# First layer's experts: TensorE's products in one fixed order, the context products in two blocks, and half of each down matrix split into high and low parts

## The chip, the cores and the metric

The program runs on one core of a Trainium2 chip. Its five engines run side by side and wait for each other on semaphores: TensorE (PE, with its weight loads as PEld), VectorE (DVE), ScalarE (ACT), GpSimd (POOL) and SyncE (SP), which here only issues transfers. The metric is the device time of one execution in microseconds (us), the median over the runs shown; less is better.

## What is computed

The reference is a two-layer network over 1024 latent tokens and 256 context tokens of width 1024. Each layer has token mixers and then an expert layer, in which each of 16 experts picks its own tokens (128 latent ones, and 32 context ones in the first layer only) and adds its result to them:

```python
aff = softmax(h @ w_router)
vals, idx = lax.top_k(aff.transpose(0, 2, 1), cap)
xg = h[idx]
hid = silu(xg @ w_gate) * (xg @ w_up)
out = (hid @ w_down) * vals
...
zeros.at[idx].add(out)
```

An expert's three matrices are 1024x512 (gate, up) and 512x1024 (down), in float32. The first layer does this for the latent and for the context tokens; the second layer needs the latent tokens alone.

## The kernel before, in words

Each expert matrix comes as two transfers of 1 MB into a ring of nine `est` tiles (`expert_w`), issued by SP in order; a transfer waits until the tile nine places earlier is free. The products of the latent tokens with gate and up are made from split operands: `split` casts a tile on ACT to a high part `ewh` (float32r) and forms the remainder `ewl` on DVE, in three buffers each; `expert_x` transposes the gathered tokens `xg` on PE (`xt`), scales them on DVE (`xm`), shifts them on POOL, and splits them into `xh` (ACT) and `xo` (DVE). `expert_up` then makes, for each half of a matrix, the twelve products `pg` of xh with ewh, xo with ewh and xh with ewl. The down products `pd` are made in float32 without a split. The 32 context tokens are multiplied in float32 with the `est` tiles themselves, in 32-column strips of the array (`pgc`, `pdc`); their four partial sums are copied to `sc` and added by products with a selection matrix (`hcp`), and the result is transposed (`hct`). `slots` finds the indices of a later expert with small products (`slp`), and POOL gathers by them (`xg`, `xgc`) and scatters the results with an addition (`x<-yo`, `c<-yc`).

The PSUM banks are dealt out by hand (`BANKS`): gate and up sums in banks 0 and 1, the two halves of the down result in 2 and 3, the transposes `xt` and `hidp` in bank 4 alone, the context sums in 5 and 6, `slp` and `xtc` in bank 7.

The order on each engine is set by a scheduler from the order in which the program is written, from the dependencies, and from its own estimate of the times: on PE it puts products of several experts between each other. `issue_after` ties an instruction behind another on its engine. After the last expert the second layer's first modulation vectors are computed (`adaln`, products `aps`), and then the second layer's `norm1` loads the rows of `c` and `x`, squares them on ACT (`sq`), and forms `h`.

Of the kernel before, what the change touches and what calls it, by code (L numbers as in the profile page):

```python
# [19 lines left out]
P = 128  # L20
# [22 lines left out]
class Kern:  # L43
# [1177 lines left out]
    def expert_x(self, l, r, ep, eng=None):  # L1221
# [6 lines left out]
        for k in range(0, KD, 4):  # L1228
            ps = self.bank("xt" if need else "xt2", [P, 4, P], F32, "xt")
            for j in range(4):  # L1230
                nc.tensor.transpose(ps[:, j], xg[:, (k + j) * P:(k + j + 1) * P], self.idf)  # L1231
# [6 lines left out]
        if need:  # L1238
# [4 lines left out]
            for c in range(2):  # L1243
                nc.tensor.transpose(ps[:, c], xgc[:, c * P:(c + 1) * P], self.idf)
# [5 lines left out]

    def expert_up(self, l, r, ep, first=False):
# [4 lines left out]
        pc, sc = None, []  # L1256

        def ctx_mm(gu, hf, st):

            nonlocal pc  # L1260
            if hf == 0:
                pc = self.bank("upc", [P, 512], F32, "pgc")
            for k in range(4):
                kk = 4 * hf + k
                nc.tensor.matmul(pc[32 * k:32 * k + 32], r["xc"][:, kk % 2, 32 * (kk // 2):32 * (kk // 2) + 32],  # L1265
                                 st[:, 512 * k:512 * k + 512], start=hf == 0, stop=hf == 1, tile_position=(0, 32 * k),
                                 skip_group_check=True)
            if hf == 1:
                t = ep.tile([P, 512], F32, name=f"sc{gu}", bufs=1)
                nc.scalar.copy(t, pc)  # L1270
                sc.append(t)
        late = []
        for gu in range(2):
            n = 0
            for hf in range(2):
                st = r[("gate", "up")[gu]][hf]
                wh, wl = r["pre"].pop(0) if r.get("pre") else self.split(self.ws, st, [P, 2048], "ew", 3)
# [5 lines left out]
                if need:  # L1283
                    late.append((gu, hf, st))
                    if len(late) > 1 * first:
                        ctx_mm(*late.pop(0))
        for x in late:
            ctx_mm(*x)
        return acc, sc

    def expert_hid(self, l, r, up, ep):
        nc = self.nc
        need = l < DEPTH - 1
        (pg, pu), sc = up
        hid = ep.tile([P, 512], F32, name="hid", bufs=1 + need)
        nc.scalar.activation(hid, pg, AF.Silu)
        nc.vector.tensor_tensor(hid, hid, pu, ALU.mult)
        ps = self.bank("xt" if need else "downc", [P, 4, P], F32, "hidp")
        for j in range(4):
            nc.tensor.transpose(ps[:, j], hid[:, j * P:(j + 1) * P], self.idf)  # L1300
        hT = ep.tile([P, 4, P], F32, name="hidT", bufs=2)
        nc.scalar.copy(hT, ps)  # L1302
        if need:

            ps = self.bank("downc", [P, 256], F32, "hcp")
# [5 lines left out]
            hc, uc = [ep.tile([64, 256], F32, name=n, bufs=1) for n in ("hidc", "upc")]  # L1311
            nc.scalar.activation(hc, ps[:64], AF.Silu)
            nc.vector.tensor_copy(uc, ps[64:])
            nc.vector.tensor_tensor(hc, hc, uc, ALU.mult)
            ps = self.bank("downc", [P, 2, 64], F32, "hct")
            for c in range(2):
                nc.tensor.transpose(ps[:, c], hc[:, P * c:P * c + P], self.idf[:64, :64])
            hcT = ep.tile([P, 2, 2, 32], F32, name="hcT", bufs=2)
            nc.vector.tensor_copy(hcT.rearrange("p h c s -> p c h s"), ps.rearrange("p c (h s) -> p c h s", h=2))
        return hT, (hcT if need else None)  # L1320

    def expert_down(self, l, r, hid, ep, g5, g5c, xl, xc):
# [6 lines left out]
        for hf in range(2):  # L1329
            st = r["down"][hf]  # L1330

            for k in range(2):
                for nn in range(2):
                    c = 1024 * k + 512 * nn
                    self.downed = nc.tensor.matmul(po[nn], hT[:, 2 * hf + k], st[:, c:c + 512],  # L1335
                                                   start=hf == 0 and k == 0, stop=hf == 1 and k == 1)
            for k in range(2):
                if need:
                    for nn in range(2):
                        o = 64 * k + 32 * nn  # L1340
                        nc.tensor.matmul(pd[o:o + 32], hcT[:, hf, k], st[:, 1024 * k + 512 * nn:1024 * k + 512 * nn + 512],
                                         start=hf == 0, stop=hf == 1, tile_position=(0, o), skip_group_check=True)
# [12 lines left out]
    def experts(self, l, xl, xc):  # L1355

        nc = self.nc
        with self.pool(f"ex{l}") as ep, self.pool(f"ws{l}") as self.ws, self.pool(f"ew3_{l}") as ew3:
# [12 lines left out]
            self.nw = 0  # L1371

# [18 lines left out]
            start(2, rs[0]["xd"])  # L1391
            for e in range(NE):
# [146 lines left out]
```

## Time and profile before

| what | value |
|---|---|
| median of 3 runs | 2729.64 us (2728.22 to 2730.44) |
| the profiled execution | 2732.13 us, span 2730.4 us, so 1.7 us lie around the span |
| PE busy | 2504.4 us (92% of the span) |
| DVE busy | 1884.3 us (69%) |
| ACT busy | 1131.4 us (41%) |
| first layer's experts on PE | first gate product at 1005.67 us, last down product from 1440.27 us on |

The shares are means over stages with different limits; the first layer's experts are about a sixth of the span. A timeline row gives the start, the time from the first start to the last end of a merged group, and in brackets how long the engine had been idle and what ended it. The ends of matmuls are modelled, so for PE the distance between the starts of two neighbouring rows says what a group took.

### The profile page before, as it was taken

How to read it: one execution, taken by the hardware profiler on the slowest of the kernel's cores; microseconds unless marked ns; L12 is line 12 of the kernel's file. 1: busy time of each engine (PE TensorE's matmuls, PEld its weight loads, DVE VectorE, ACT ScalarE, POOL GpSimd, SP SyncE). 2: the span in 40 equal slices, each digit the busy share in tenths (PEclk: the TensorE clock that was granted, in tenths of full speed). 3: DMA queues.
4: the chain of work that ended last, by engine and by line, in shares of the span. 5: the costliest groups of instructions: out<-in, count | busy, mean ns of one | idle time of the engine just before them, and what ended most of it. 6: DMA issues, size and time to landing. Idle time of an engine off the chain costs nothing.

```text
span 2730.4 us, 55190 instructions
## 1 busy us (share of the span) xinstructions
PE 2504.4 (92%) x21959; PEld 1906.9 (70%) x21959; DVE 1884.3 (69%) x4046; ACT 1131.4 (41%) x1878; POOL 669.3 (25%) x621
## 2 busy tenths in 40 slices
PE   7999999998999979999996999999958899589997
PEld 4998887894677855555554988778844677367664
DVE  4258887857666586777754368787858874787874
ACT  4224433324554534444434334333314554345452
POOL 1000000035444633333311000000045532222241
PEclk9999999998999979999998999999979999789999
DMA  7332324247354948888887332423176355889994
GB/s 281 102 108 71 114 68 123 66 138 243 113 160 135 349 151 278 281 280 279 283 280 212 94 105 74 124 84 89 49 200 225 94 163 183 300 281 370 377 376 127
DMA packets 347936, 507.12 MB, mean 186 GB/s; under 512 B 53380, under 2 KB 203072, under 8 KB 346592
## 3 DMA queue, kind: packets, MB, share of 16 engines
q1 hardware_dynamic: 336416, 465.85, 50.4%
q0 software_dynamic: 11264, 37.75, 5.9%
q8 instruction: 173, 2.83, 0.4%
q14 instruction: 83, 0.68, 0.1%
HBM read 410.10 MB, written 94.90 MB: 185 GB/s over the span
## 4 chain that ended last, share of the span: by engine, by line
PE 67%; DVE 18%; DMA 5%; issue 4%; ACT 3%; POOL 2%; SPq 1%; POOLq 0%; DVEq 0%; ACTq 0%
PE pg L1280 13%; PE pj L277 12%; PE pd L1335 8%; PE pj L288 8%; PE po L828 6%; PE nao L786 3%; PE pgc L1265 2%; PE npt L762 2%; PE sA L733 1%; DVE Kt L375 1%; PE aps L157 1%; DVE Kt L376 1%; DVE Qt L378 1%; PE hl L365 1%; PE xt L1231 1%
## 5 line engine op out<-in xcount | busy, mean ns | idle before, releaser
L1182 DVE TENSOR_TENSOR ewl<-est,ewh 128x2048 fp32r<-128x2048 f32 x126 | 298.1, 2371 | 109.7 <-ACT ewh L1178 108.6
L1178 ACT CAST ewh<-est 128x2048 fp32r<-128x2048 f32 x128 | 243.4, 1905 | 170.9 <-PE pg L1280 130.5
L277 PE MATMUL pj<-hl,whi 128*128 128x320 f32 (+2 forms) x912 | 310.2, 340 | 0.0
L277 PE MATMUL pj<-hh,whi 128*128 128x320 f32 (+2 forms) x912 | 309.9, 340 | 0.0
L277 PE MATMUL pj<-hh,wlo 128*128 128x320 f32 (+2 forms) x912 | 308.7, 339 | 0.0
L288 PE MATMUL pj<-whi,hh 128*128 128x256 f32 x960 | 277.8, 290 | 4.5 <-ACT nev L566 4.1
L288 PE MATMUL pj<-whi,hl 128*128 128x256 f32 x960 | 276.8, 291 | 0.8 <-DVE hl L239 0.8
L288 PE MATMUL pj<-wlo,hh 128*128 128x256 f32 x960 | 275.5, 288 | 0.0
L1335 PE MATMUL pd<-est,hidT 128*128 128x512 f32 x512 | 232.2, 596 | 2.1 <-ACT hidT L1302 2.1
L288 PEld LDWEIGHTS pj<-whi,hh 128*128 128x128 f32 x960 | 186.0, 194 | 8.8 <-ACT nev L566 5.2
L288 PEld LDWEIGHTS pj<-wlo,hh 128*128 128x128 f32 x960 | 185.9, 194 | 2.2 <-issue 1.3
L288 PEld LDWEIGHTS pj<-whi,hl 128*128 128x128 f32 x960 | 184.6, 194 | 3.5 <-issue 1.3
L277 PEld LDWEIGHTS pj<-hh,whi 128*128 128x128 f32 x912 | 172.2, 189 | 13.7 <-issue 0.9
L277 PEld LDWEIGHTS pj<-hl,whi 128*128 128x128 f32 x912 | 172.2, 189 | 13.5 <-issue 1.9
L277 PEld LDWEIGHTS pj<-hh,wlo 128*128 128x128 f32 x912 | 172.1, 189 | 13.0 <-issue 1.1
L1335 PEld LDWEIGHTS pd<-est,hidT 128*128 128x128 f32 x512 | 95.2, 189 | 110.7 <-issue 103.3
L265 DVE TENSOR_TENSOR wlo<-wst,whi 128x1024 fp32r<-128x1024 f32 (+1 forms) x72 | 75.2, 1058 | 131.7 <-ACT whi L264 130.6
L1280 PE MATMUL pg<-ewh,xh 128*128 128x512 f32 x512 | 156.8, 424 | 3.1 <-ACT xh L1235 3.0
L752 POOL TENSOR_SCALAR S<-S,sm 128x768 f32<-128x768 f32 (+2 forms) x108 | 108.6, 1007 | 188.3 <-DVE sm L751 166.8
L1280 PE MATMUL pg<-ewl,xh 128*128 128x512 f32 x512 | 147.7, 404 | 0.0
L1280 PE MATMUL pg<-ewh,xo 128*128 128x512 f32 x512 | 142.3, 398 | 2.1 <-DVE xo L1236 2.1
L750 ACT ACTIVATE S<-S,mn 128x768 f32<-128x768 f32 (+2 forms) x108 | 98.6, 913 | 85.2 <-DVE mn L745 79.6
(369 smaller groups left out, 5560.9 us busy)
## 6 DMA issues: line engine op xcount, KB each, us to landing
est<-in_w_exp_gate_dram SPq DMA_DIRECT2D x64, 1024.0 KB
est<-in_w_exp_up_dram SPq DMA_DIRECT2D x64, 1024.0 KB
est<-in_w_exp_down_dram SPq DMA_DIRECT2D x64, 1024.0 KB
wm<-in_w_mod_dram SPq DMA_DIRECT2D x80, 512.0 KB
wst<-in_w_in_dram SPq DMA_DIRECT2D x88, 256.0 KB
pna<-nev SPq DMA_DIRECT2D x180, 64.0 KB
wos<-in_w_out_dram SPq DMA_DIRECT2D x42, 256.0 KB
mst<-mix SPq DMA_DIRECT2D x32, 320.0 KB
```

Source lines behind the costliest of these rows:

```text
L265: nc.vector.tensor_tensor(b, c, a, ALU.subtract)
L277: nc.tensor.matmul(ps[:, :cn], sel(a(k)), b[:, k, c0:c0 + cn], start=n == 0, stop=n == 3 * KD - 1)
L288: nc.tensor.matmul(ps[:, :2 * P], b[:, k, t * P:(t + 1) * P], a(k).rearrange("p a n -> p (a n)"), start=n == 0, stop=n == 3 * KD - 1)
L750: nc.scalar.activation(S[:, :w], S[:, :w], AF.Exp, scale=-1.0, bias=mn[:, 1:2], accum_out=sm[:, 0:1])
L752: nc.gpsimd.tensor_scalar(S[:, :w], S[:, :w], sm[:, 1:2], 1.0, ALU.mult, ALU.mult)
L762: nc.tensor.transpose(pt[:kn, i], S[:, c:c + kn], self.idf)
L786: nc.tensor.matmul(po[64 * X:64 * X + 64, gi], V[:kn, tt, 64 * X:64 * X + 64], PT[X][:kn, i], start=i == 0, stop=i == len(ch) - 1, tile_po ...
L828: nc.tensor.matmul(ps, a, b, start=n == 0, stop=n == len(ops) - 1)
L1178: nc.scalar.copy(hi, src)
L1182: nc.vector.tensor_tensor(lo[:, :m], src[:, :m], hi[:, :m], ALU.subtract)
L1280: nc.tensor.matmul(acc[gu], a[:, 4 * hf + k], b[:, 512 * k:512 * k + 512], start=n == 0, stop=n == 3 * KD - 1)
L1335: self.downed = nc.tensor.matmul(po[nn], hT[:, 2 * hf + k], st[:, c:c + 512], start=hf == 0 and k == 0, stop=hf == 1 and k == 1)
```

## The change

It has four parts, all in the expert layer, and they act in the first layer only (`need` is true there). First, a context manager `then` ties each product and transpose to the one traced before it, so that PE takes them in the order in which they are written. Second, the order written is a new one: within an expert gate, the context's gate and up products together, up; then the context's sums; then the context's down products, the transposes of the expert after next, the latent down products, and the transposes of the hidden values. For the first expert the context's block follows up. Third, the second of the two down tiles is split as gate and up are, and its four float32 products become twelve float32r products, with the hidden values split too (`hTh`, `hTl`). Fourth, banks change: the context's up sums go to bank 6, `hcp` and `hct` to bank 5, and the context's hidden tile is transposed in full width.

```diff
+    @contextmanager
+    def then(self, on=True):
...
+        def after(f):
+            def g(*a, **k):
+                with tc.issue_after(self.pel.ins) if self.pel is not None else nullcontext():
+                    self.pel = f(*a, **k)
+                return self.pel
+            return g
+        nc.tensor.matmul, nc.tensor.transpose = after(mm), after(tr)
...
+        with self.then(need):
+            prods(0)
+            if need and not first:
+                ctx_mm(0)
+                ctx_mm(1)
+            prods(1)
+            if need and first:
+                ctx_mm(0)
+                ctx_mm(1)
...
+            hh, hl = [ep.tile([P, 2, P], F32R, name=n, bufs=2) for n in ("hTh", "hTl")]
+            nc.scalar.copy(hh, hT[:, 2:])
+            nc.vector.tensor_tensor(hl, hT[:, 2:], hh, ALU.subtract)
...
         if need:
+            hTh, hTl = self.hTs
+            wh, wl = self.split(self.ws, r["down"][1], [P, 2048], "ew", 3)
             pd = self.bank("downc", [P, 512], F32, "pdc")
...
+            if mid:
+                mid()
...
+                        if need and hf == 1:
+                            for i, (a, b) in enumerate(((hTh, wh), (hTl, wh), (hTh, wl))):
+                                self.downed = nc.tensor.matmul(po[nn], a[:, k], b[:, c:c + 512], start=False,
+                                                               stop=k == 1 and i == 2)
+                            continue
...
+            hid = self.expert_hid(l, rs[0], up, ep)
+            if need:
+                pc = self.expert_ctx(up[1])
+                hidc = self.expert_ctx_hid(pc, ep)
             for e in range(NE):
                 if e + 3 <= NE:
                     start(e + 3, rs[e + 1]["xd"])
-                hid = self.expert_hid(l, rs[e], up, ep)
-                if e + 2 < NE:
+                if not need and e + 2 < NE:
                     self.expert_x(l, rs[e + 2], self.xp)
                 if e + 1 < NE:
                     up = self.expert_up(l, rs[e + 1], ep)
-                self.expert_down(l, rs[e], hid, ep, g5, g5c, xl, xc)
+                    if need:
+                        pc = self.expert_ctx(up[1])
+                more = lambda: self.expert_x(l, rs[e + 2], self.xp) if e + 2 < NE else None
+                self.expert_down(l, rs[e], (hid, hidc if need else None), ep, g5, g5c, xl, xc, more)
+                if e + 1 < NE:
+                    hid = self.expert_hid(l, rs[e + 1], up, ep)
+                    if need:
+                        hidc = self.expert_ctx_hid(pc, ep)
```

In the order of the changed program every product within `then` bears the line of the wrapper, L1265. The first place is PE around the transposes `xt` of the expert after next, in the middle of the first layer. Before:

```order
L1341 MATMUL pdc<-est,hcT 32x512 x8
L1148 LDWEIGHTS O
L1148 MATMUL slp<-pay,O 128x5
L1148 LDWEIGHTS O
L1148 MATMUL slp<-pay,O 128x5
L1231 MATMUL xt<-idf,xg 128x128 x4
L1280 MATMUL pg<-ewh,xh 128x512
L1280 MATMUL pg<-ewh,xo 128x512 x4
L1280 MATMUL pg<-ewl,xh 128x512 x4
```

And now:

```order
L1265 MATMUL hcp<-sc_13109,sel 32x256 x2
L1265 MATMUL hcp<-sc_13120,sel 32x256 x2
L1265 MATMUL pdc<-est,hcT 32x512 x8
L1265 MATMUL xt<-idf,xg 128x128 x8
L1265 MATMUL xtc<-idf,xgc 128x128 x2
L1265 MATMUL pd<-est,hidT 128x512 x4
L1265 MATMUL pd<-ewh,hTh 128x512
L1265 MATMUL pd<-ewh,hTl 128x512
L1265 MATMUL pd<-ewl,hTh 128x512
```

Before, gate and up products stood between the two groups of four transposes; now the eight follow each other, though both groups use bank 4. The second place is DVE at the same point of an expert. Before (`A` is the scale of the tokens):

```order
L1154 SCALAR_TENSOR_TENSOR ix<-sl,pdiv 128x1
L1156 SCALAR_TENSOR_TENSOR ixd<-sl,pdiv 128x1
L1233 TENSOR_TENSOR xm<-xt,A_12256 128x512
L1351 TENSOR_TENSOR yd<-pdc,yd 64x512
L1352 SCALAR_TENSOR_TENSOR yc<-yd,val,g5c 64x512
```

And now:

```order
L1182 TENSOR_TENSOR ewl<-est,ewh 128x2048
L1349 TENSOR_TENSOR hid<-hid,pg 128x512
L1182 TENSOR_TENSOR ewl<-est,ewh 128x2048
L1333 COPY upc<-hcp 64x256
L1234 TENSOR_TENSOR xm<-xt,A_12256 128x512
L1404 TENSOR_TENSOR yd<-pdc,yd 64x512
L1334 TENSOR_TENSOR hidc<-hidc,upc 64x256
L1405 SCALAR_TENSOR_TENSOR yc<-yd,val,g5c 64x512
```

Two splits (those of the next gate), the product `hid` and a copy now stand directly ahead of the first `xm`. The third place is PE at the first expert, after the small products `slp`. Now:

```order
L1265 MATMUL xtc<-idf,xgc 128x128 x2
L1265 MATMUL xt<-idf,xg 128x128 x8
L1265 MATMUL xtc<-idf,xgc 128x128 x2
L1265 MATMUL pg<-ewh,xh 128x512 x4
L1265 MATMUL pg<-ewh,xo 128x512 x4
```

Before, at this place:

```order
L1280 MATMUL pg<-ewl,xh 128x512 x4
L1231 MATMUL xt<-idf,xg 128x128 x4
L1280 MATMUL pg<-ewh,xh 128x512 x4
L1244 MATMUL xtc<-idf,xgc 128x128 x2
L1280 MATMUL pg<-ewh,xo 128x512 x4
```

The first expert's products `pg` used to start ahead of the second expert's transposes; now they stand behind them.

## Rows read from the trace of the kernel before

**Rows 1.** Windows: stretch, its us, five engines' busy us, PE clock, DMA share, GB/s.

```profile
1000.00:1020.00 20.00, 16.39 (x67) 12.13 (x67) 18.00 (x32) 7.08 (x6) 5.15 (x3) 0.65 0.21 66
1200.00:1250.00 50.00, 50.00 (x265) 27.57 (x263) 36.57 (x48) 22.27 (x23) 18.29 (x12) 1.00 0.83 282
```

**Rows 2.** Chain in order of time: start, us, what; first and last of eleven.

```profile
1100.55 4.29 PE pd L1335 x10
...
1372.87 4.29 PE pd L1335 x10
```

**Rows 3.** Timeline of PE, one expert of the middle.

```profile
1182.09 4.45 PE L1335 MATMUL pd<-est,hidT 128*128 128x512 f32 x10
1186.47 1.92 PE L1265 MATMUL pgc<-est,xct 128*32 128x512 f32 x16
1188.32 2.84 PE L1335 MATMUL pd<-est,hidT 128*128 128x512 f32 x6
...
1198.71 0.64 PE L1231 MATMUL xt<-idf,xg 128*128 128x128 f32 x4
1199.10 0.48 PE L1280 MATMUL pg<-ewh,xh 128*128 128x512 f32 x1
1199.41 1.08 PE L1280 MATMUL pg<-ewh,xo 128*128 128x512 f32 x4
1200.33 1.07 PE L1280 MATMUL pg<-ewl,xh 128*128 128x512 f32 x4
...
1204.93 0.64 PE L1309 MATMUL hcp<-sc,sel 128*32 128x256 f32 x8
```

**Rows 4.** Timelines of ACT, DVE and POOL, the same expert.

```profile
1200.53 1.91 ACT L1178 CAST ewh<-est 128x2048 fp32r<-128x2048 f32 x1 [1.17 <-PE pg L1280]
...
1183.01 0.43 DVE L1313 COPY upc<-hcp 64x256 f32<-64x256 f32 x1
...
1199.38 0.69 DVE L1233 TENSOR_TENSOR xm<-xt,A 128x512 f32<-128x512 f32 x1
...
1202.78 2.29 DVE L1182 TENSOR_TENSOR ewl<-est,ewh 128x2048 fp32r<-128x2048 f32 x1
1204.99 0.69 DVE L1236 TENSOR_TENSOR xo<-xm,xh 128x512 fp32r<-128x512 f32 x1
...
1202.92 3.48 POOL L1170 DMA_INDIRECT c<-yc,ixd  x1 [0.83 <-DVE val L1160]
```

**Rows 5.** Timelines of PE and POOL, first two experts.

```profile
1002.08 1.12 PE L1231 MATMUL xt<-idf,xg 128*128 128x128 f32 x4 [0.78 <-DVE xm L1233]
...
1005.67 3.75 PE L1280 MATMUL pg<-ewh,xh 128*128 128x512 f32 x8
...
1018.67 0.60 PE L1231 MATMUL xt<-idf,xg 128*128 128x128 f32 x4
...
1012.51 1.69 POOL L1165 DMA_INDIRECT xg<-h2l,ix  x1 [0.30 <-DVE xo L1236]
1017.52 2.83 POOL L1165 DMA_INDIRECT xgc<-h2c,ix  x1 [3.33 <-DVE ixd L1156]
```

**Rows 6.** Timelines of PE, POOL, SP and ACT, from the last expert to the second layer.

```profile
1440.27 7.13 PE L1335 MATMUL pd<-est,hidT 128*128 128x512 f32 x16 [0.73 <-ACT hidT L1302]
...
1448.65 4.49 PE L157 MATMUL aps<-est,sT 128*32 128x512 f32 x40
1453.07 0.33 PE L1317 MATMUL hct<-idf,hidc 64*128 64x64 f32 x2
...
1455.89 1.90 PE L1341 MATMUL pdc<-est,hcT 128*32 128x512 f32 x16
...
1461.07 1.43 POOL L1170 DMA_INDIRECT c<-yc,ixd  x1 [10.49 <-DVE yc L1352]
...
1466.43 0.97 SPq L221 DMA_DIRECT2D x<-c  x2
...
1472.35 1.06 ACT L224 ACTIVATE sq<-x 128x1024 f32<-128x1024 f32 x1 [0.24 <-DMA x<-c]
...
1477.42 1.94 ACT L236 ACTIVATE h<-ps,mt,ab 128x256 f32<-128x256 f32 x4
```

More of the change, by code (lines that the diff above doesn't have):

```diff
@@ L1255, in expert_up, with prods @@
         acc = [self.bank("up", [P, 512], F32, "pg") for _ in range(2)]
[L1256 to L1273, printed above, removed]
+        sc = []
+        def prods(gu):
             n = 0
             for hf in range(2):
-                st = r[("gate", "up")[gu]][hf]
-                wh, wl = r["pre"].pop(0) if r.get("pre") else self.split(self.ws, st, [P, 2048], "ew", 3)
+                wh, wl = r["pre"].pop(0) if r.get("pre") else self.split(self.ws, r[("gate", "up")[gu]][hf], [P, 2048],
+                                                                         "ew", 3)
                 for a, b in ((xh, wh), (xo, wh), (xh, wl)):
@@ L1282, in expert_up, with ctx_mm, expert_ctx @@
                         n += 1
[L1283 to L1288, printed above, removed]
+        def ctx_mm(gu):
+            pc = self.bank(("upc", "downc")[gu], [P, 512], F32, "pgc")
+            for hf in range(2):
+                st = r[("gate", "up")[gu]][hf]
+                for k in range(4):
+                    kk = 4 * hf + k
+                    nc.tensor.matmul(pc[32 * k:32 * k + 32], r["xc"][:, kk % 2, 32 * (kk // 2):32 * (kk // 2) + 32],
+                                     st[:, 512 * k:512 * k + 512], start=hf == 0, stop=hf == 1, tile_position=(0, 32 * k),
+                                     skip_group_check=True)
+            t = ep.tile([P, 512], F32, name=f"sc{gu}", bufs=1)
+            nc.scalar.copy(t, pc)
+            sc.append(t)
+        with self.then(need):
+            prods(0)
[6 more added lines that the diff above has]
+                ctx_mm(1)
         return acc, sc
-    def expert_hid(self, l, r, up, ep):
+    def expert_ctx(self, sc):
         nc = self.nc
[L1293 to L1305, printed above, removed]
+        ps = self.bank("upc", [P, 256], F32, "hcp")
+        with self.then():
             for i, t in enumerate(sc):
@@ L1318, in expert_hid, with expert_ctx_hid @@
[L1318 to L1322, printed above, removed]
+        return ps
+    def expert_ctx_hid(self, ps, ep):
+        nc = self.nc
+        hc, uc = ep.tile([P, 256], F32, name="hidc", bufs=1), ep.tile([64, 256], F32, name="upc", bufs=1)
+        nc.scalar.activation(hc, ps, AF.Silu)
+        nc.vector.tensor_copy(uc, ps[64:])
+        nc.vector.tensor_tensor(hc[:64], hc[:64], uc, ALU.mult)
+        pt = self.bank("upc", [P, 2, P], F32, "hct")
+        with self.then():
+            for c in range(2):
+                nc.tensor.transpose(pt[:, c], hc[:, P * c:P * c + P], self.idf)
+        hcT = ep.tile([P, 2, 2, 32], F32, name="hcT", bufs=2)
+        nc.vector.tensor_copy(hcT.rearrange("p h c s -> p c h s"), pt[:, :, :64].rearrange("p c (h s) -> p c h s", h=2))
+        return hcT
@@ L1323, in expert_down @@
+    def expert_down(self, l, r, hid, ep, g5, g5c, xl, xc, mid=None):
         nc = self.nc
@@ new lines, in expert_down @@
+            if mid:
+                mid()
+        po = [self.bank("down", [P, 512], F32, "pd") for _ in range(2)]
+        with self.then(need):
+            for hf in range(2):
+                for k in range(2):
+                    for nn in range(2):
+                        c = 1024 * k + 512 * nn
+                        if need and hf == 1:
[3 more added lines that the diff above has]
+                            continue
+                        self.downed = nc.tensor.matmul(po[nn], hT[:, 2 * hf + k], r["down"][hf][:, c:c + 512],
+                                                       start=hf == 0 and k == 0, stop=hf == 1 and k == 1)
```

62 lines of the change are left out of this document (40 added, 22 removed).

## The prediction

> **What bounds the kernel now.** I read the page first (PE 92% of the span), then windows of 20 and 50 us over the first layer's experts, the chain of waits for the period, and the timelines of one expert and of both ends. In the middle of these experts PE is busy for 50.00 of 50 us at a granted clock of 1.00, while DVE has 36.57, ACT 22.27 and POOL 18.29, and the DMA engines are used to 0.83 at 282 GB/s [rows 1]. So PE sets the pace there, and nothing waits for weights. In the chain the same group `pd` comes at 1100.55 and, ten experts on, at 1372.87 [rows 2]: the period is 272.32 / 10 = 27.23 us. At the start it is otherwise: PE has 16.39 of 20 us and a clock of 0.65 [rows 1]. At the end no expert follows, and the path runs through the last scatters and the loads of the second layer's rows. So three places are to be costed: the start, the period (14 of them matter), and the crossing into layer two.
>
> **The period, PE's own work.** Sixteen `pd` records are the eight down products; ten take from 1182.09 to 1186.47, 0.438 each [rows 3], so 7.01 us in all. After the change eight records stay (3.50) and twelve float32r products come. These cost as `pg` does: four from 1199.41 to 1200.33, 0.23 each [rows 3], together 2.76. That saves 0.75 us. A lone `pg` behind the transposes took 0.31 (1199.10 to 1199.41) against 0.23 [rows 3], so a change of kind costs about 0.08; the fixed order has some four fewer, -0.3, while the small `slp` products, which are not tied, fall into the context block (+0.15 estimated). PE's work per expert is then 27.23 - 0.75 - 0.30 + 0.15 = 26.33 us. Were PE never to wait, 15 experts would gain some 13 us.
>
> **The new wait.** Both transposed halves `xt` use bank 4, and nothing stands between them now: the second four wait until DVE's `xm` has read the first. In the middle it does not occur before, since `pg` lay between. And `xm` will not start at once: DVE's order now has two `ewl`, `hid` and `upc` ahead of it. I count from the end of the xo products of up's first half, which frees the buffer of the next `ewh`:
>
> - ACT's cast starts 0.20 later and takes 1.91 (1200.33 to 1200.53; [rows 3, 4]).
> - `ewl` 2.21: its start to the next one's, 1202.78 to 1204.99 [rows 4]. Back to back, DVE's 2.29 overlaps the next by 0.08.
> - `hid`, of the shape of `xm` (0.69), taken as 0.61; the second `ewl` 2.21; `upc` 0.43 less 0.08; `xm` 0.69 [rows 4].
>
> At the start, where two groups of `xt` did follow each other, the wait is seen: 0.78 us on DVE `xm` [rows 5].
>
> The sum of the list is 2.11 + 2.21 + 0.61 + 2.21 + 0.35 + 0.69 = 8.18 us. In that time PE has four wl products (0.92), up's second half (12 x 0.23 = 2.76), `hcp` 0.64, `pdc` 1.90 and the first `xt` 0.64, each of these three less some 0.05 since their ends are modelled [rows 3, 6]: 6.71 us. PE waits 1.5 us per expert. The lower bound is a DVE that is free: then the wait is about 0.95 (the 0.78 of the start with the transposes' own tail). The upper bound is 2.1, if both `ewl` run without overlap and the cast is late by half a microsecond. I take 1.5, because DVE's order is a fixed queue and each term is a row. The period is 26.33 + 1.5 = 27.85, about **27.9 us** (27.3 to 28.4), +0.65 over 14 experts: about +9 us.
>
> The Trainium skill, "Perfetto Trace Analysis", section "Matmuls", says that independent matmul groups should rotate through different PSUM banks, so that the reading out of one overlaps the next. It speaks against the two halves back to back in one bank, and the 0.78 us of [rows 5] agrees with it. By that rule alone, without DVE's queue, the wait would be the 0.95 of the lower bound.
>
> **What is hidden.** The split of the down tile adds a cast of 1.91 on ACT and an `ewl` of 2.29 on DVE per expert [rows 4]. ACT has 22.27 of 50 busy and DVE 36.57 [rows 1], about 19.9 of 27.23 for DVE; with 2.3 and `hTl` more (a quarter of a tile's width, at most 0.5) it is 22.7 of 27.9. The d1 split can be done while PE is at gate and up, some ten us ahead of its use; if its cover went, PE would wait up to 4.2 us per expert, which no load supports. Five splits go through three buffers instead of four; each buffer comes free at least 9 us before its next products. Weights: 282 GB/s at a share of 0.83 leaves room for 340, and a longer period asks for less. The `est` tile of the split is held until its `pdc` and the split are through, no longer than before.
>
> **The start.** The order now ties the second expert's transposes ahead of the first `pg`. Their rows `xg` are gathered by an instruction on POOL that starts at 1012.51, and they stood ready at 1018.67, where `xt` ran without a wait [rows 5]. POOL's place for that gather doesn't move. `xgc`, which started at 1017.52 after 3.33 us of waiting for its index [rows 5], follows at once now, as the index products no longer stand behind `pg`. So the first half starts near 1018.2, then `xm` 0.69 and the second half 0.60, and `pg` starts near 1020.3 instead of 1005.67 [rows 5]. If the gathers land 1 us sooner or 3 later, so does it. Of the 48 `pg`, the first dozen go at the low level of the clock (0.47 each, 3.75 for eight, against 0.23 [rows 3, 5]; the clock was 0.65 on average in this stretch [rows 1]): 11.0 + 2.9 + 0.4. Two context blocks follow, 1.85 each (1186.47 to 1188.32, [rows 3]), to 1038.3. Then come the copy of the sums, `hcp` 0.64, silu, `upc` 0.43, the product and `hct` 0.33 [rows 3, 4, 6], about 4.1 with waits that aren't covered (2.1 is the bare sum with 0.69 for the copy; 6 if ACT and DVE are at splits). The second expert's gate starts near 1042.4.
>
> **The crossing.** The last down product ends at 1042.4 + 14 x 27.9 - 0.5 (the first period has no earlier down ahead) + 24.8 (the fifteenth has neither `xt` nor `slp`, nor the wait) + 9.7 (the sixteenth: 1.4 wait for `hcT`, 1.85 `pdc`, 6.45 `pd`) = **1467**. Before it was 1440.27 + 7.1 = 1447.4 [rows 6]. So PE is 20 us later there, but most of it comes back. Before, the last `hct` and `pdc` stood behind the 40 `aps` (1448.65, 1453.07, 1455.89), the scatter `c` ran at 1461.07, the load of these rows at 1466.43, `sq` at 1472.35 and `h` at 1477.42, 30 us after the last `pd` [rows 6]. Now `pdc` stands ahead of `pd`, the context rows are scattered during `pd`, and the path is that of `x`: its scatter goes 1.1 after the last `pd`, and as with `c` (1461.07 to 1466.43) its rows can be loaded 5.4 later; from there to `h` it took 10.99 at most (1466.43 to 1477.42), and 0.97 + 5.07 at least [rows 6]. So `h` is 12.5 to 17.5 behind the last `pd`. I take 15.7, as SP's queue has the load of the modulation vectors ahead of `x`'s rows, and those wait for `aps` (4.4 us) and the sums behind it. `h` starts at 1482.7, +5.3; with the weights of the first projection queued behind those loads I take +6.
>
> **The sum.** +6.0 on the profiled execution of 2732.13, i.e. 2738.1. That execution is 2.49 above the median of 2729.64, so on the runs' scale 2735.6: **2736 us**. Counted otherwise: start and crossing give back what they take to about -3, and the period adds 9. The second layer is untouched but for the order of some small products; +-3 us unpriced. 0.2%, 5.5 us, is about what a measurement of this kernel can tell from no change, so the forecast lies just outside of it.
>
> **Rivals.**
> - *The wait is shorter than what is saved (faster).* Place: DVE before `xm`. If `xm` gets ahead of an `ewl`, or the cast starts sooner, 2.2 us leave the chain and only a remnant of 0.45 stays: period 26.8, 14 x 1.1 = 15.4 less than forecast: 2720; without any wait 2714. It decides from a wait of about 0.65 down (2736 - 14 x 0.85 = 2724). For it: PE's own work falls by 0.9 for certain. Against it: DVE's order is fixed, and even a free DVE costs 0.95 by the row.
> - *The wait is at its floor (no change).* 0.95: period 27.3, 2736 - 14 x 0.6 = 2727.6, within 0.2%.
> - *A second wait per expert (slower still).* POOL's scatter `c` stands between the two additions to `xm`. It took 3.48 us beside a split on DVE [rows 4] and 1.43 alone [rows 6]. If it takes the long form here each time, the second half's `xh` and `xo` come 2 us later, where about 1 is to spare: +1.0 per expert, 2750. The Trainium skill, "SBUF — State Buffer", section "Who interferes with whom", says that DVE and GpSimd share a port pair under an exclusive lock, which fits the two durations.
> - *The fixed order does nothing* since the scheduler had it so: excluded by the order, which differs at all three places.
>
> **How the numbers follow.** Forecast 0.55 (2729 to 2743: the wait from 1.1 to 2.0, crossing and start +-3), second wait 0.18, shorter wait 0.17, floor 0.10. The range runs from 2718, which takes in most of the shorter wait, to 2750. Faster by over 0.2% (below 2724) is the shorter wait and a little of the floor: 0.20. Within 0.2% (to 2735): the floor's rest and the lower half of the forecast, 0.33. Slower: the forecast's upper half and the second wait, 0.47.
>
> **What would show it.** The period between equal `pd` groups: 27.9; 26.8 or less means that the wait is gone, 28.9 that there are two. PE idle 1.5 us ahead of the second `xt`, ended by DVE `xm`, with two `ewl` just before. `pg` of the first expert at 1020, the second's gate at 1042. The last `pd` at 1467 and `h` 15 to 16 us later. The prediction is wrong if DVE comes to `xm` early, if the gathers of the start are late, or if d1's split is late, which would show as PE waiting for DVE `ewl` ahead of `pd`.

## The result, and the profile after

The changed kernel takes 2765.8 us in the median of 4 runs (2762.62 to 2766.76), the kernel before 2730.04: a ratio over all runs of 1.0117 (95% interval 1.0103 to 1.0132; the plain quotient of the two medians is 1.0131). It is slower, in the direction of the forecast, but by 36 us in the medians and 32 by the ratio, where 6 were predicted. The profiled execution has a span of 2765.0 us against 2730.4.

The windows of the middle of the first layer's experts, as in [rows 1]: stretch, its us, busy us of PE, PEld, DVE, ACT and POOL, PE clock, DMA share, GB/s.

```profile
1150.00:1200.00 50.00, 46.58 (x248) 27.60 (x248) 41.93 (x54) 23.18 (x23) 18.38 (x12) 0.97 0.79 249
1200.00:1250.00 50.00, 46.39 (x259) 29.44 (x257) 40.38 (x47) 24.73 (x25) 15.82 (x11) 1.00 0.83 281
```

PE no longer is busy throughout, and in one of the two windows its clock is below 1. The chain of waits, which in [rows 2] ran through PE alone, now leaves it once per expert for DVE:

```profile
1181.22 7.72 PE pd L1265 x20
...
1207.03 2.20 DVE ewl L1182
1211.34 6.21 PE pd L1265 x20
...
1235.62 2.20 DVE ewl L1182
...
1413.14 7.83 PE pd L1265 x20
```

From one `ewl` of the chain to the next it is 28.59 us, the period, where 27.23 stood before and 27.85 was forecast. Three of the `pd` groups (the third starts at 1297.15) take 7.7 to 7.8 us instead of 6.2: around each of them a window of 50 us reads a granted clock of 0.97 (of the two levels, 1.2 and 2.4 GHz, the lower for a part of it), where all windows of these experts read 1.00 before.

The timeline of PE, two experts of the middle and one near the end, with ACT and DVE behind it:

```profile
1208.02 0.66 PE L1265 MATMUL xt<-idf,xg 128*128 128x128 f32 x4
1210.47 0.66 PE L1265 MATMUL xt<-idf,xg 128*128 128x128 f32 x4 [1.79 <-DVE xm L1234]
...
1223.96 2.76 PE L1265 MATMUL pgc<-est,xct 128*32 128x512 f32 x18
1226.65 0.20 PE L1148 MATMUL slp<-pay,O 128*128 128x5 bf16 x2
1226.79 1.92 PE L1265 MATMUL pgc<-est,xct 128*32 128x512 f32 x14
1228.63 1.20 PE L1265 MATMUL pg<-ewh,xh 128*128 128x512 f32 x4
...
1427.06 3.64 PE L1265 MATMUL pgc<-est,xct 128*32 128x512 f32 x32
1430.63 1.20 PE L1265 MATMUL pg<-ewh,xh 128*128 128x512 f32 x4
...
1432.57 1.07 PE L1265 MATMUL pg<-ewl,xh 128*128 128x512 f32 x4
...
1438.58 0.66 PE L1265 MATMUL xt<-idf,xg 128*128 128x128 f32 x4
1441.04 0.65 PE L1265 MATMUL xt<-idf,xg 128*128 128x128 f32 x4 [1.81 <-DVE xm L1234]
...
1432.77 1.91 ACT L1178 CAST ewh<-est 128x2048 fp32r<-128x2048 f32 x1 [1.42 <-PE pg L1265]
...
1434.71 2.29 DVE L1182 TENSOR_TENSOR ewl<-est,ewh 128x2048 fp32r<-128x2048 f32 x1 [4.22 <-ACT ewh L1178]
1436.92 0.68 DVE L1349 TENSOR_TENSOR hid<-hid,pg 128x512 f32<-128x512 f32 x1
1437.52 2.28 DVE L1182 TENSOR_TENSOR ewl<-est,ewh 128x2048 fp32r<-128x2048 f32 x1
1439.84 0.43 DVE L1333 COPY upc<-hcp 64x256 f32<-64x256 f32 x1
1440.29 0.69 DVE L1234 TENSOR_TENSOR xm<-xt,A 128x512 f32<-128x512 f32 x1
```

Two things are to be seen. First, the forecast wait: the second `xt` starts 2.45 us behind the first, 1.8 of it idle, and DVE works through `ewl`, `hid`, `ewl` and `upc` without a pause before it comes to `xm`. Second, one that the prediction had priced at 0.15 us: the context block of the middle, with two `slp` in it, lasts from 1223.96 to 1228.63, 4.67 us; the same 32 products without `slp`, near the end, last from 1427.06 to 1430.63, 3.57 us.

Start and crossing, the rows that answer to [rows 5, 6], from the timelines of POOL, PE, SP and ACT:

```profile
1016.02 1.87 POOL L1165 DMA_INDIRECT xg<-h2l,ix  x1 [0.30 <-DVE ix L1154]
...
1021.22 1.12 PE L1265 MATMUL xt<-idf,xg 128*128 128x128 f32 x4 [2.90 <-DMA xg<-h2l,ix]
1024.32 2.06 PE L1265 MATMUL pg<-ewh,xh 128*128 128x512 f32 x4
...
1044.99 2.06 PE L1265 MATMUL pg<-ewh,xh 128*128 128x512 f32 x4
...
1443.39 1.46 POOL L1170 DMA_INDIRECT c<-yc,ixd  x1 [1.22 <-DVE yc L1405]
...
1481.53 7.07 PE L157 MATMUL aps<-est,sT 128*32 128x512 f32 x64
...
1488.66 0.80 SPq L221 DMA_DIRECT2D x<-c  x2
...
1498.50 1.93 ACT L236 ACTIVATE h<-ps,mt,ab 128x256 f32<-128x256 f32 x4
...
1502.45 0.79 PE L288 MATMUL pj<-whi,hh 128*128 128x256 f32 x2 [1.28 <-ACT whi L264]
```

And behind the crossing, in the second layer, which the change doesn't touch: the products `atp` (three groups of modulation vectors, the last in the second layer's attention) and the router's products `lgk` behind that attention, first of before, then of the changed kernel (the last numbers ahead of the shapes are first and last start):

```profile
L171 PE MATMUL atp<-idf,ms x24: 272/273/422, 32.9 to 2109.9; 128*128 128x128 f32 x24
...
L942 PE MATMUL lgk<-hT,wm x128: 272/273/297, 2314.5 to 2352.2; 128*32 128x128 f32 x128
```

```profile
L171 PE MATMUL atp<-idf,ms x24: 272/273/328, 34.7 to 2138.2; 128*128 128x128 f32 x24
...
L942 PE MATMUL lgk<-hT,wm x128: 272/273/297, 2349.6 to 2387.2; 128*32 128x128 f32 x128
```

At the second layer's first projection `pj` the changed kernel is 23.5 us behind (1502.45 against 1478.99 before), at the last `atp` 28.3, and at `lgk` 35.1. So a third of the loss arises in code that both kernels share. (The last `atp` stands 33 products further ahead of `lgk` in the changed kernel's order, so the part up to it and the part behind it are best taken together: `pj` to `lgk` takes 11.6 us more than before.)

### The profile page after: what moved, and what is told of

It is laid out like the page before. It is cut to its first block, busy times and chain, and to the rows that moved or that the text cites. A ratio compares the mean times of both kernels' runs of the same rounds, so it can differ in the third digit from the quotient of the medians.

```text
span 2765.0 us, 55363 instructions
## 1 busy us (share of the span) xinstructions
PE 2506.5 (91%) x22023; PEld 1937.4 (70%) x22023; DVE 1934.0 (70%) x4078; ACT 1171.2 (42%) x1910; POOL 669.1 (24%) x621
## 4 chain that ended last, share of the span: by engine, by line
PE 64%; DVE 18%; DMA 7%; ACT 4%; issue 3%; POOL 2%; SPq 2%; POOLq 0%; ACTq 0%; DVEq 0%
PE pj L277 12%; PE pj L288 7%; PE pg L1288 6%; PE po L828 6%; PE pg L1265 5%; PE pd L1265 4%; PE pd L1394 4%; PE nao L786 3%; PE pgc L1265 2%; DVE ewl L1182 2%; PE npt L762 2%; PE aps L157 2%; DMA wm<-in_w_mod_dram 2%; PE sA L733 1%; ACT ewh L1178 1%
## 5 line engine op out<-in xcount | busy, mean ns | idle before, releaser
L1182 DVE TENSOR_TENSOR ewl<-est,ewh 128x2048 fp32r<-128x2048 f32 x142 | 330.8, 2334 | 126.5 <-ACT ewh L1178 124.9
L1178 ACT CAST ewh<-est 128x2048 fp32r<-128x2048 f32 x144 | 274.2, 1908 | 166.6 <-PE pg L1288 81.8
L1235 POOL TENSOR_TENSOR xm<-xm,mt 128x512 f32<-128x512 f32 x60 | 80.8, 1356 | 208.8 <-DVE xm L1234 194.9
L157 PE MATMUL aps<-wm,sT 128*32 128x512 f32 x320 | 85.0, 672 | 41.3 <-DMA wm<-in_w_mod_dram 41.3
L786 PE MATMUL nao<-PT,nav 128*64 128x128 f32 (+1 forms) x1296 | 114.9, 286 | 5.8 <-ACT PT L765 5.3
L354 ACT COPY kz<-Kt 64x320 f32<-64x320 f32 x120 | 55.0, 467 | 150.4 <-DVE Kt L375 131.0
L1394 PE MATMUL pd<-est,hidT 128*128 128x512 f32 x256 | 115.1, 592 | 0.7 <-ACT hidT L1355 0.7
```

The lines of the kernel that those rows point to most:

```text
L157: nc.tensor.matmul(ps[32 * j:32 * j + 32], self.sT[:, k, :], w[j], start=k == 0, stop=k == KD - 1, tile_position=(0, 32 * j))
L786: nc.tensor.matmul(po[64 * X:64 * X + 64, gi], V[:kn, tt, 64 * X:64 * X + 64], PT[X][:kn, i], start=i == 0, stop=i == len(ch) - 1, tile_po ...
L1178: nc.scalar.copy(hi, src)
L1182: nc.vector.tensor_tensor(lo[:, :m], src[:, :m], hi[:, :m], ALU.subtract)
L1394: self.downed = nc.tensor.matmul(po[nn], hT[:, 2 * hf + k], r["down"][hf][:, c:c + 512], start=hf == 0 and k == 0, stop=hf == 1 and k == 1)
```

## The experiments

Each ratio is to the kernel before in runs of the same chip, whose median was 2727.7 to 2733.78 us on the four chips; a difference between two other kernels is across chips unless the text says otherwise. Kernels whose name begins with "halves" differ from the changed kernel, the rest as said. The period is taken from `hidp` to `hidp` over ten experts.

**The halves of xt kept apart.** The second four transposes go behind the four float32 `pd` products.

```diff
-            if mid:
-                mid()
+            if mid:
+                mid((0,))
...
             for hf in range(2):
+                if need and hf == 1:
+                    mid((4,))
```

> The changed kernel with the second group of four xt transposes moved behind the four float32 pd products, so that PE has other work while xm reads the first group out of bank 4; nothing else differs. Theory 1 (the wait for xm is what lengthens the period, 1.81 us idle per expert in the changed kernel, and the drops of the clock inside the experts follow from PE's idling): no idle time ahead of the second xt, period 28.59 down to about 26.7, no 3.4 us drop of the clock between the second expert and the last, time 2765.8 - 14 x 1.9 - 3 x 1.5 = about 2735. Rival (the fixed order only moves the wait: the next thing PE needs, hTl, the split of the down tile or ewl of the next gate, is late by as much): period stays above 28, time above 2757.

Measured: 2714.24 us, a ratio of 0.9949 (0.9932 to 0.9965) to before: faster than both kernels. PE's timeline:

```profile
1117.92 0.60 PE L1266 MATMUL hidp<-idf,hid 128*128 128x128 f32 x4
...
1212.60 0.66 PE L1266 MATMUL xt<-idf,xg 128*128 128x128 f32 x4
...
1213.31 3.60 PE L1266 MATMUL pd<-est,hidT 128*128 128x512 f32 x8
1216.75 0.60 PE L1266 MATMUL xt<-idf,xg 128*128 128x128 f32 x4
...
1226.37 3.64 PE L1266 MATMUL pgc<-est,xct 128*32 128x512 f32 x32
1229.94 1.21 PE L1266 MATMUL pg<-ewh,xh 128*128 128x512 f32 x4
...
1373.09 0.60 PE L1266 MATMUL hidp<-idf,hid 128*128 128x128 f32 x4
```

No wait is left, and the period is (1373.09 - 1117.92) / 10 = 25.52. The rival falls: nothing else is late. But it gains 51.6 us on the changed kernel (49 when each is held against before on its own chip) where theory 1 expected 30, since the period fell by 3.07 and not by 1.9. The wait is 2.1 of it (counted from start to start, the two `xt` groups cost 2.95 us per expert before this edit and 0.85 after). The other 1.0 is the context block: the scheduler, which places the free `slp`, now puts them elsewhere, and the block takes 3.57 us. The drops of the clock are gone with the wait. What two different banks for the two halves would bring was not tried.

**No split.** All down products in float32 again, order and banks as changed.

```diff
-            wh, wl = self.split(self.ws, r["down"][1], [P, 2048], "ew", 3)
...
-                        if need and hf == 1:
-                            for i, (a, b) in enumerate(((hTh, wh), (hTl, wh), (hTh, wl))):
...
-            hh, hl = [ep.tile([P, 2, P], F32R, name=n, bufs=2) for n in ("hTh", "hTl")]
...
```

> The changed kernel with all down products in float32 again (no split of the second down tile, no hTh and hTl); order and banks as changed. Theory 1 (the split saves PE 0.8 us per expert but its fifth place in the ring of three ew buffers makes the casts of the next gate wait for up's last products, so that two ewl stand ahead of xm): pd 7.0 instead of 6.2, but the casts go early and the wait for xm falls from 1.8 to about 0.9; period about 28.3 to 28.5, time 2758 to 2765. Rival (the split is a plain gain of PE and the wait comes from the order alone): the wait stays at 1.8, period 29.4, time about 2777.

Measured: 2774.72 us, 1.0169 (1.0141 to 1.0196). The rival holds:

```profile
1214.18 0.86 PE L1265 MATMUL xt<-idf,xg 128*128 128x128 f32 x4 [1.80 <-DVE xm L1234]
```

The wait is as long as with the split, and the period is 29.2 us, or 30.9 where the clock drops, which it does in five periods. A cast goes as soon as the xo products three splits earlier have freed its buffer, with four splits per expert as with five, so two `ewl` fall ahead of `xm` in either case. The wait does not come from the split.

**Free start.** The second expert's transposes are written behind the first expert's products.

```diff
-            self.expert_x(l, rs[1], self.xp)
...
             with self.tc.issue_after(slotted.ins), self.tc.issue_after(self.listed.ins):
                 up = self.expert_up(l, rs[0], ep, True)
+            if need:
+                self.expert_x(l, rs[1], self.xp)
```

> The changed kernel with the second expert's transposes written behind the first expert's products instead of ahead of them; the rest differs in nothing. Theory 1 (the start costs because the first pg stand behind transposes that wait for their gathers): the first pg starts some 13 to 15 us earlier than in the changed kernel, the second expert's gate 8 to 12 us earlier, time about 2754 to 2758. Rival (the start is bound by the gathers and by the second expert's own transposes, so that the second gate starts when it did): time within 4 us of 2765.8.

Measured: 2762.32 us, 1.0127 (1.011 to 1.0144), 3.5 us below the changed kernel across chips; against before, each on its own chip, the two are about equally slow.

```profile
1010.94 2.04 PE L1265 MATMUL pg<-ewh,xh 128*128 128x512 f32 x4
...
1036.66 2.06 PE L1265 MATMUL pg<-ewh,xh 128*128 128x512 f32 x4
```

The first `pg` starts 13.4 us earlier than in the changed kernel, the second expert's gate 8.3, but this execution was 7.0 us ahead already at the router's first `ctp` (981.3 against 988.3), in code that has the same order in both. Of the start itself 1.3 us remain. The rival holds: the transposes, the sums and `hct` that now stand between the two experts take what the early start gives.

**The split alone**, in the kernel before.

```diff
+            wh, wl = self.split(self.ws, r["down"][1], [P, 2048], "ew", 3)
...
+                    if need and hf == 1:
+                        for i, (a, b) in enumerate(((hTh, wh), (hTl, wh), (hTh, wl))):
```

> The kernel before with the split of the second down tile alone (twelve float32r products in place of four float32 ones, hidden values split too); the scheduler orders everything, no banks change. Theory 1 (PE is the bound and the split takes 0.75 us of its work per expert, its cast and its ewl hidden): period 27.23 to 26.5, time 2730 - 11 = about 2719. Rival (five splits in a ring of three buffers make ACT and DVE late, or the scheduler's order gets worse, and PE waits as it does in the changed kernel): period 27.2 or more, time 2730 or more.

Measured: 2740.6 us, 1.0042 (1.0025 to 1.0059): slower. The windows of this kernel over 300 us of the experts:

```profile
1100.00:1400.00 300.00, 300.00 (x1629) 166.31 (x1628) 237.45 (x300) 152.44 (x154) 99.29 (x64) 1.00 0.83 277
```

PE is busy for 300 of 300 us at a clock of 1, and yet the period of these ten experts is (1388.92 - 1109.51) / 10 = 27.94 against 27.23. The down products `pd` fall from 7.08 to 6.51 us per expert, but the scheduler breaks the other products up: `pgc` comes in 4.5 groups per expert and costs 4.53 us (3 groups and 3.85 before), `pg` comes in 7.3 groups in place of 5 and costs 12.11 in place of 11.77, `pdc` costs 2.17 in place of 1.86. Neither theory had this: PE doesn't wait, it works worse. The order isn't the same in all experts: from the first `hidp` to the last, 15 periods, this kernel takes 414.4 us and before 412.8, so the split's saving is used up and little more. Of the 9.6 us by which the profiled execution is longer, 2.3 are there ahead of the experts and 7.2 lie in the second layer (below).

**A small part of the change that should cost nothing**: the full-width `hct` alone (with the silu ahead of it over 128 rows), in the kernel before.

```diff
-            ps = self.bank("downc", [P, 2, 64], F32, "hct")
+            ps = self.bank("downc", [P, 2, P], F32, "hct")
...
-                nc.tensor.transpose(ps[:, c], hc[:, P * c:P * c + P], self.idf[:64, :64])
+                nc.tensor.transpose(ps[:, c], hc[:, P * c:P * c + P], self.idf)
```

> The kernel before with one small part of the change alone: the context's hidden tile is transposed in full width (hct 128x128 in place of 64x64). In the first layer this is some 0.1 us per expert of PE's work or nothing, but the scheduler's order of the second layer's attention preparation becomes the one of the changed kernel (on SP two loads of qk ahead of four wm in place of qk, wm, qk, three wm). Theory 1 (the changed kernel's second layer, about 10 us longer than before, is longer because of that order): this kernel is 6 to 10 us slower than before, all of it behind the point where the second layer prepares the second pair of heads. Rival (the second layer's 10 us come from the first layer's late end, from another phase of clock drops, or are chance): within 3 us of before.

Measured: 2741.0 us, 1.0036 (1.0022 to 1.005): slower by some 10 us. The windows from the second layer's first `pj` to its first `lgk`, of before, of this kernel and of the changed one, in the columns of [rows 1]:

```profile
1478.99:2314.54 835.55, 766.64 (x8375) 636.23 (x8375) 592.35 (x1392) 336.60 (x664) 163.54 (x165) 0.97 0.41 125
```

```profile
1479.01:2324.36 845.35, 773.03 (x8376) 641.03 (x8376) 590.21 (x1392) 336.72 (x664) 161.18 (x165) 0.97 0.41 124
```

```profile
1502.45:2349.60 847.15, 776.43 (x8369) 643.20 (x8369) 588.70 (x1385) 336.79 (x662) 162.40 (x165) 0.96 0.41 124
```

Its first layer is as short as before's (`h` at 1477.41 against 1477.42). From `pj` to `lgk` it takes 9.8 us more than before, and the order on the engines there, the attention's above all, is nearly the changed kernel's. Theory 1 holds, and for the change as a whole it means that most of the second layer's loss has nothing to do with how long the experts take. The windows also show how this order lengthens the stretch: PE is busy 6.4 us longer for the same products, and 9.8 us in the changed kernel. In the trace's records of the granted clock the lower level holds for 43 us of this stretch before, 55 here and 64 in the changed kernel; half of the added time, 6 and 10 us, is an estimate of what that costs at most. So most of the loss is the granted clock, and the rest is PE idling. The changed kernel's order gives no fixed loss, though: by their profiled executions, halves apart and free start, with the same order, are 9.1 and 5.1 us longer than before from `pj` to `lgk`.

**The slot products kept out of the context block**, in the changed kernel.

```diff
-                if e + 3 <= NE:
-                    start(e + 3, rs[e + 1]["xd"])
...
                     up = self.expert_up(l, rs[e + 1], ep)
+                    if need and e + 3 <= NE:
+                        self.tie = self.ctxl
+                        start(e + 3, rs[e + 1]["xd"])
+                        self.tie = None
```

with each `slp` behind `self.tie`, the last product of the context block.

> The changed kernel with the slot products slp of the expert three ahead kept behind the context block (they go behind up and between the two xt groups); nothing else is moved by hand. Theory 1 (two slp products in the middle of the strip products pgc break the groups of four that run side by side, 4.54 us per block in place of 3.57): pgc falls to 3.6 us, the period by about 1 us, time about 2752. Rival (the longer block is a wait for banks or data that only happens to stand beside the slp): pgc stays at 4.5, time within 4 us of 2765.8.

Measured: 2740.43 us, 1.0041 (1.0026 to 1.0055).

```profile
1212.15 3.64 PE L1266 MATMUL pgc<-est,xct 128*32 128x512 f32 x32
1215.72 1.20 PE L1266 MATMUL pg<-ewh,xh 128*128 128x512 f32 x4
...
1224.36 0.20 PE L1149 MATMUL slp<-pay,O 128*128 128x5 bf16 x2
1226.27 0.66 PE L1266 MATMUL xt<-idf,xg 128*128 128x128 f32 x4 [1.72 <-DVE xm L1235]
```

The block takes 3.57 us again with the wait still there, as theory 1 had it. The period is (1369.52 - 1096.81) / 10 = 27.27, 1.3 below 28.59: 1.0 is the block, and the rest small pieces: two `slp` now run inside the wait, the other eight no longer stand within a run of `pg`, and the wait is 0.1 shorter. The gain is 25 us across chips and not 14. The profiled executions differ by 28.3: 3.3 are there ahead of the experts, 20.4 arise from there to the second layer's first projection (14 x 1.3 = 18, and no drop of the clock is left in the middle), and 4.6 behind it, where the order is another one.

**xm ahead of the splits on DVE**, in the changed kernel: the next gate's two `ewl` are tied behind the first `xm`.

```diff
+            with self.tc.issue_after(self.low.ins) if self.low is not None else nullcontext():
+                nc.vector.tensor_tensor(lo[:, :m], src[:, :m], hi[:, :m], ALU.subtract)
...
+                self.low = self.xm0 if need and not first and gu == 0 else None
```

> The changed kernel with the next gate's two ewl tied behind the first xm on DVE; transposes stay back to back in bank 4. Theory 1 (the wait is DVE's queue, 8.5 us of ewl, hid, ewl and upc from the end of up's first xo products, and the bank alone costs only about 0.95): the second xt waits 0.8 to 1.0 us in place of 1.81, period about 27.6 to 27.8, time 2750 to 2754. Rival (bank 4 itself or the late upc sets it): the wait stays above 1.5 us, time within 5 us of 2765.8, or slower as the next gate's ewl is late.

Measured: 2792.23 us, 1.0226 (1.0211 to 1.0241).

```profile
1214.47 0.65 PE L1268 MATMUL xt<-idf,xg 128*128 128x128 f32 x4 [0.79 <-DVE xm L1235]
...
1228.02 2.05 PE L1268 MATMUL pg<-ewh,xo 128*128 128x512 f32 x4 [2.16 <-DVE xo L1240]
```

The wait ahead of the second `xt` falls to 0.79, the floor of the start's row in [rows 5]. So the other microsecond was DVE's queue. But the two `ewl` now stand ahead of the second `xm`, `xo` is late, and PE waits 2.16 us at the next gate, behind which `pg` runs at half clock (four in 1.84 us in place of 0.91). The period is (1405.68 - 1098.60) / 10 = 30.71. The time contradicts the expectation, the place of the wait confirms it. The context block of this kernel has `slp` in it too, eight of them, but behind 24 strip products:

```profile
1231.63 2.78 PE L1268 MATMUL pgc<-est,xct 128*32 128x512 f32 x24
1234.35 0.36 PE L1148 MATMUL slp<-pay,O 128*128 128x5 bf16 x8
1234.63 1.07 PE L1268 MATMUL pgc<-est,xct 128*32 128x512 f32 x8
```

Here the 32 strip products take 3.72 us (2.72 and 1.00 from start to start), not 4.54. So a product over the full array in the block is not by itself what costs; in the changed kernel the two `slp` come behind 18 strip products, the last two of which run singly.

**Halves apart, and no split.** Both edits above.

> The changed kernel with the xt halves apart (as in halves_apart) and all down products in float32. Theory 1 (with PE never waiting the split is worth its PE time, 7.0 - 6.2 = 0.8 us per expert): period 25.5 + 0.8 = 26.3, time 2714 + 13 = about 2727, if the second layer keeps its length. Rival (the split's cast and ewl cost elsewhere as much as PE saves): period 25.5 to 25.8, time 2714 to 2718.

Measured: 2727.46 us, 0.9987 (0.9978 to 0.9996). The period is (1382.91 - 1120.99) / 10 = 26.19, 0.67 above that with the split; theory 1 holds. This kernel makes the same products as the one before but for the wider `hct`, and PE waits in neither; the order, with the banks that go with it, takes the period from 27.23 to 26.19. By kind of product, per expert, `pg` falls from 11.77 to 11.39 us, `pgc` from 3.85 to 3.57, `pd` from 7.08 to 6.87, `hct` from 0.27 to 0.14 (the width), `hcp` from 0.57 to 0.46.

**Halves apart, with the narrow hct of before**, for another order of the second layer.

```diff
-        pt = self.bank("upc", [P, 2, P], F32, "hct")
+        pt = self.bank("upc", [P, 2, 64], F32, "hct")
...
-                nc.tensor.transpose(pt[:, c], hc[:, P * c:P * c + P], self.idf)
+                nc.tensor.transpose(pt[:, c], hc[:, P * c:P * c + P], self.idf[:64, :64])
```

> halves_apart with the context's hidden tile transposed in 64 columns again, as in the kernel before. In the first layer nothing but some 0.1 us per expert can change; the scheduler's order of the second layer becomes a third one, unlike that of before and of the changed kernel. Theory 1 (the order of the second layer is worth some 8 us by itself, whatever the experts do): experts as in halves_apart, period 25.5, and a second layer that differs from that of halves_apart by several us in either direction; time between 2704 (as short as before's) and 2720. Rival (that stretch is long whenever the first layer ends at another time): the same 8 us as in halves_apart, 2714 within 2 us.

Measured: 2726.66 us beside 2733.78 for before on this chip, 0.9971 (0.9961 to 0.9981), so 0.2% less gain than with the full width. The period is 25.74, 0.22 more (in full width, `hct` and the `hidp` ahead of it cost 0.2 less), and the second layer is 3 us longer still in the one execution profiled. Theory 1 holds in that the order alone changes that stretch; that it would get as short as before's it did not.

## Why the prediction was wrong

The span grew by 34.6 us, where 6.0 were forecast. By places: 3.6 are there already at the router's first `ctp`, 19.9 arise from there to the second layer's first projection, and 11.1 behind it. Against the forecast, the period is 14 x 0.74 = 10.4 too long, the drops of the clock add 5, the crossing 3 and the second layer 11.1; the start, with the first and last experts, gives back some 4.

**Ahead of the experts, 3.6 us, forecast 0.** The order on all engines is the same in both kernels there. The other nine kernels, with the same order too, are 3.4 us ahead to 5.6 behind at this point. So the 3.6 lie within the spread of executions and aren't counted as an effect of the change.

**The start: right.** `pg` of the first expert at 1020.3, the second gate at 1042.4 were forecast; less the 3.6, they are at 1020.7 and 1041.4, with PE waiting for the gather `xg` and for `xm` as written.

**The period: the mechanism right, two terms mis-sized.** The forecast was 26.33 of work and 1.5 of waiting, together 27.85; measured were 26.5 and 2.1, together 28.6.
- The wait's chain was forecast at 8.18 us and took 8.47 (1432.57 to 1441.04); the work beside it was put at 6.71 and took 6.37 (8.47 less the wait of 2.1, which is counted from start to start; PE's idle time in the rows is 1.8). Each is off by some 0.3 us, and the difference of two near numbers carries both errors in full: 14 x 0.6 = 8.4 us of time. In the chain, the prediction took off overlaps that `upc` and `xm` did not have: from the second `ewl` to `upc` it is 2.32 us (forecast 2.21), from `upc` to `xm` 0.45 (0.35). That the queue of DVE and not the bank alone sets the wait was right (`xm` put first cuts it to 0.79).
- The slot products in the context block were put at 0.15 us; they cost 1.0, since they break groups of strip products that run side by side. The fixed order was put at -0.3, for fewer changes of kind, and brings about -1.0, some 0.1 of it by the wider `hct` (26.19 against 27.23). The two errors hid each other in the sum; that the work came out almost right, 26.5, was luck.

**The drops of the clock, 5 us: not in the forecast at all.** With PE idling 1.8 us once per expert, the clock came down three times in the middle, and such a period is 1.7 us longer. No split and free start, with the same wait, have five each. The kernels without a wait have none, but neither has the one in which two `slp` run inside the wait, so what decides isn't settled by these runs. The first and the last two experts were some 3 us shorter than forecast.

**The crossing.** The last `pd` to `h`: 15.7 forecast, 17.0 measured (1481.5 to 1498.50), inside of the bounds. The prediction had named both the scatter of `x` and SP's queue behind `aps`; the second decided, and its price was too low: it counted 40 `aps`, 4.4 us, but 64 run behind the last `pd`, from 1481.53 to 1488.6, and SP's first load of rows comes at 1488.66, right behind them. To the first projection it took 20.95 where 18 were forecast.

**The second layer: the step that failed most.** It was called untouched, "+-3 us unpriced". It cost 11.1 (11.6 up to `lgk`, of which half a microsecond comes back behind it), and the experiment with `hct` alone, which leaves the experts as they were, loses 9.8 there by the scheduler's order: every edit of the first layer that was run let it settle the second layer in another way, and all ten profiled executions after an edit are longer there than before's, by 5 to 16 us. Most of it is the granted clock, as the windows at that experiment show. The amount is uncertain by some us, for executions with the changed kernel's own order read 5.1, 9.1 and 11.6. Why that order brings the clock down more often stays open.

**The rivals.** The second wait per expert, given 0.18, came nearest with its 2750, but for another reason: the scatter `c` took 1.4 to 1.5 us in every expert, nothing like 3.48, and PE never waited for it. It no longer stood beside a split: `xm`, `xct` and `xo` ran beside it, while before it took 3.48 us wherever a whole `ewl` lay beside it. So the lock on a shared port that the Trainium skill, "SBUF — State Buffer", section "Who interferes with whom", describes was not put to the test by the change. The rule of the Trainium skill's page "Perfetto Trace Analysis", section "Matmuls", on independent groups in different banks, agrees with the 0.79 that is left when DVE comes to `xm` first, and with halves apart, where other work stands between the two groups in bank 4 and the wait is gone; two banks, which is what the rule asks for, were not tried. The rest of the wait is the queue in front of the evacuating engine, which the rule doesn't speak of. The prediction's "without any wait 2714" is the time of halves apart to the microsecond, but by luck: it stands on a period of 26.3 and an untouched second layer, and that kernel has 25.52 and a second layer 9 us longer.

## What to carry to other kernels

Put independent work between two groups that share a PSUM bank, and look at what stands ahead of the reading instruction in its engine's queue: here the bank alone cost 0.8 us and the queue another one. A PE that is busy 100% of a window may still lose 3 to 4% to the order of its products (27.23 us against 26.19 here), so compare orders by the time per kind of product, not by the busy share. Where a scheduler orders the whole program, an edit in one stage can change the order of another; compare the stages behind the edit, and hold a near-nothing edit against it before crediting the edit itself.

## What the runs showed of the hardware

The context products stand in 32-column strips of the array, and the trace shows four of them starting within 0.02 us of each other, a group of four every 0.43 us: 32 records take 3.57 us. Two small products over the full array in the changed kernel come behind 18 of them, the last two of which run singly, and the 32 then take 4.54 us beside the 0.14 of the small ones (also without the split, and with the free start). Where eight small ones come behind 24, six full groups, the 32 take 3.72. So most of the price is that of the broken groups. The Trainium skill, "TensorE: Matmul & The Clock Gate", section "Part 3: Packing small matmuls — row/col tiling", says that products in different tiles of the array run at the same time and end in the order of issue; the trace agrees with the first part, and the price of a group that is broken up is what these runs add.

The drop of the clock after idling of 1.8 us costs 1.5 us in the group behind it (a `pd` group of 7.72 against 6.21); in the window of 50 us around it the granted clock reads 0.97. It came in three of the changed kernel's periods and in five each of no split's and free start's, in none of the kernel whose wait of 1.72 has two `slp` in it. Where `xm` is first and PE idles 2.16 us ahead of `pg`, windows of 50 us read 0.93 to 0.97 all through the experts.
